# Two-operand work moved from GpSimd to VectorE in a two-layer hybrid diffusion block

## The chip, the cores and the metric

The kernel runs on one core of one Trainium2 chip. The metric is the device time of one execution in microseconds (us). The engines are called as the profile calls them: PE is TensorE (PEld its weight loads), DVE is VectorE, ACT is ScalarE, POOL is GpSimd, and SP is the engine whose queue issues most DMAs.

## What is computed

The reference runs two layers over 512 latent tokens and 256 context tokens of width 1024, each with two sub-layers that are scaled, shifted and gated by a conditioning vector:

```python
for layer in range(DEPTH):
    mod = jax.nn.silu(c) @ w_ada[layer] + b_ada[layer]        # mod_c the same from c_ctx
    sh1, sc1, gt1, sh2, sc2, gt2 = jnp.split(mod[:, None, :], 6, axis=-1)
    h = rmsnorm(x, g_norm1[layer]) * (1 + sc1) + sh1
    p = jnp.split(h @ w_in[layer], SPLIT_POINTS, axis=-1)
    ya, ya_c = window_attention(p[0:3], pc[0:3], sink_a[layer], cos, sin, need_ctx)
    yb, yb_c = dense_attention(p[3:6], pc[3:6], g_q_b[layer], g_k_b[layer], cos, sin, need_ctx)
    ym, ym_c = mlstm_mixer(p[6:11], pc[6:11], ...)
    yd, yd_c = mamba_mixer(p[11:16], pc[11:16], ...)
    x = x + gt1 * (jnp.concatenate([ya, yb, ym, yd], axis=-1) @ w_out[layer])
    h2 = rmsnorm(x, g_norm2[layer]) * (1 + sc2) + sh2
    x = x + gt2 * sq_relu_ffn(h2, w_ff1[layer], w_ff2[layer])
return rmsnorm(x, g_final)
```

The context stream goes through the same weights; in layer 1 it is only read.

## The kernel before

Activations lie with features on the 128 partitions and tokens along the free dimension. Every large product is made of three matmuls in a fast float32 format: weight and activation are each split into a rounded part and a remainder (wh and wl, h and hl, ah and al), and wh·h, wh·hl and wl·h are summed. The weights come in pieces of 256 KB (`wload`, line 165: raw piece wraw by DMA, wh by ACT, wl by DVE).

The helpers matter for reading the profile. `mm` (line 96) issues matmuls, `act` (line 104) ACT's work, and `tt`, `ts` and `stt` (lines 107, 111 or 112, 115) issue DVE's, so that many operations share a line and are told apart by the names of their tiles. What goes to POOL is written out as `G.` at its place and has a line of its own. The order on each engine is made by a scheduler from the written order, the dependencies and priorities; each engine then takes its list in order.

The stages, with their times in the profile: conditioning and first projections of layer 0 (to 66 us), windowed attention A filled with projections, the Mamba branch D, the mLSTM branch C (to about 390), dense attention B, filled with the output projection (to 506), the first feed-forward (to about 1036); then layer 1 in the same order, with its feed-forward from 1442 to about 1795. While a branch works in small steps, a generator (`Stream.fill`) puts matmuls of the next projections between them, by credits that are fixed numbers.

The places that the change touches:

- `ada_step` (line 301) makes the second layer's conditioning during the first feed-forward, one of 24 column blocks at a time. Four pieces of w_ada (tile adar, from the five ta buffers that are shared with the products adap) are loaded on SP's queue, ACT scales each row by silu(c) into adap, POOL adds them into acc (line 317), adds its two halves (line 319), and for the 16 blocks that need c alone cuts the sum into three bf16 pieces together with ACT (lines 325 and 327). `ada_finish` sums over the partitions on PE and adds the bias on DVE (tile mod). The whole step is written at the lowest priority.
- `norm_chunk` (line 402): with pool=True, every second chunk gets its shift on ACT, a rounded copy on ACT, and its remainder hl on POOL (line 408).
- `rotate` (lines 627 to 639), the rotary embedding: four ACT copies make the swapped tile qs, POOL multiplies it by the sines (line 633), DVE multiplies by the cosines, POOL adds (line 638). With g it serves branch B, without g branch A.
- `Rms` (line 360) collects sums of squares, on DVE or POOL (line 371); `row` makes a reciprocal root (`rsq`, line 184) and spreads it over the partitions with matmuls.
- `c_norm` (line 1369): the mLSTM's reciprocal roots ssC, on POOL; `c_fin` uses them (line 1376).
- The skip product of branch D (tile ysk, line 1140), on POOL.
- `whole` (line 1511): in layer 1, after the first of eight feed-forward blocks, eight products x·row of full width on POOL, then ACT and the split into h2.
- In `ffn2` the PSUM results (tiles bulk and mx, two buffers each) are added to x by DVE (x<-bulk,mod,x).

## Time and profile before

| what | value |
|---|---|
| median of 3 runs | 1813.33 us (1811.78 to 1813.99) |
| the profiled execution | 1813.98 us |
| its span, first to last instruction | 1812.2 us |
| mean granted clock of PE | 0.986 |
| POOL busy | 372.5 us, 21% of the span |
| of it ada_step's adds, halves and pieces (lines 317, 319, 325, 327) | 143.4 + 28.7 + 10.8 + 12.3 = 195.2 us |
| read from HBM | 172.51 MB, mean 98 GB/s |

A group of instructions is shown as line, engine, operation, output<-inputs, shapes, count, then busy us and mean ns of one, then the engine's idle time just ahead of them and who ended it. A line of the waits is: engine and tile that waited, <- who released it, total us, times, longest us. A line of the chain is start us, length us, engine, tile. A window row is PE, PEld, DVE, ACT and POOL busy (instructions), granted clock, DMA share and GB/s. PE's ends are modelled.

### The profile page before, as it was taken

The page shows a single profiled execution, that of the slowest core. Times are in us where ns is not written, and L with a number is a line of the kernel's source. Part 1 is how long each engine was busy: PE and PEld are TensorE (multiplying, and loading weights), DVE is VectorE, ACT ScalarE, POOL GpSimd, SP SyncE. Part 2 cuts the span into 40 slices and gives each one's busy share as a digit, 9 for nine tenths or more (in the row PEclk, how much of TensorE's full clock was granted, in tenths as well). Part 3 has the DMA queues.
Part 4 walks back from the last instruction along what each step waited for, and adds up shares of the span by engine and source line. Part 5 has one row for each costly group of instructions (what it writes and reads, how often), then busy time and mean ns, then how long its engine had stood idle before and what let it go on. Part 6 is the DMA issues. An engine that isn't in the chain of part 4 may idle for free.

```text
span 1812.2 us, 29981 instructions
## 1 busy us (share of the span) xinstructions
PE 1737.6 (96%) x11178; PEld 1505.2 (83%) x11178; DVE 1158.1 (64%) x2485; ACT 900.8 (50%) x2004; POOL 372.5 (21%) x454
## 2 busy tenths in 40 slices
PE   7999999989999999999999999999989999999997
PEld 4897998778788888888888888888868888888887
DVE  4677664588867557456456566875579884444445
ACT  4655634555666455344344455663456663333334
POOL 1300121430025344133133431012140210000001
PEclk9999999999999999999999999999999999999999
DMA  9323443241033233333333412133212132222221
GB/s 346 103 94 102 141 144 106 71 149 36 13 112 111 94 122 108 103 117 99 105 122 99 140 59 75 42 95 94 71 53 73 53 100 93 94 94 93 96 96 65
DMA packets 98833, 180.36 MB, mean 100 GB/s; under 512 B 10752, under 2 KB 19840, under 8 KB 98688
## 3 DMA queue, kind: packets, MB, share of 16 engines
q1 hardware_dynamic: 97536, 176.88, 30.2%
q0 software_dynamic: 1152, 1.57, 0.5%
q8 instruction: 88, 1.44, 0.3%
q14 instruction: 57, 0.47, 0.1%
HBM read 172.51 MB, written 4.33 MB: 98 GB/s over the span
## 4 chain that ended last, share of the span: by engine, by line
PE 75%; DVE 7%; ACT 5%; POOL 5%; DMA 4%; issue 3%; SPq 0%; POOLq 0%; ACTq 0%; DVEq 0%
PE bulk L96 36%; PE s L96 29%; PE mx L96 8%; PE mx L757 2%; DMA MB<-drows 1%; DVE wl L107 1%; ACT qs L104 1%; POOL acc L317 1%; DMA adar<-in_wada_dram 1%; ACT wh L104 1%; DMA CB<-drows 1%; DVE x L115 1%; POOL qs L633 1%; DVE m L721 0%; ACT pr L104 0%
## 5 line engine op out<-in xcount | busy, mean ns | idle before, releaser
L107 DVE TENSOR_TENSOR wl<-wraw,wh 128x512 fp32r<-128x512 f32 (+1 forms) x392 | 288.3, 742 | 138.4 <-ACT wh L104 130.6
L104 ACT ACTIVATE wh<-wraw 128x512 fp32r<-128x512 f32 (+1 forms) x392 | 239.1, 619 | 254.6 <-PE bulk L96 130.1
L96 PE MATMUL s<-h,wh 128*128 128x512 f32 (+2 forms) x848 | 291.7, 346 | 1.1 <-ACT pr L104 1.1
L96 PE MATMUL s<-hl,wh 128*128 128x512 f32 (+2 forms) x848 | 281.6, 345 | 0.2 <-DVE hl L115 0.2
L96 PE MATMUL s<-h,wl 128*128 128x512 f32 (+2 forms) x848 | 251.3, 346 | 2.3 <-DVE wl L107 2.3
L317 POOL TENSOR_TENSOR acc<-acc,adap 128x512 f32<-128x512 f32 x96 | 143.4, 1499 | 404.1 <-ACT acc L104 382.5
L96 PE MATMUL bulk<-ah,wh 128*128 128x512 f32 (+1 forms) x576 | 217.9, 378 | 4.4 <-DVE mod L107 3.7
L96 PE MATMUL bulk<-ah,wl 128*128 128x512 f32 (+1 forms) x576 | 216.1, 375 | 0.0
L96 PE MATMUL bulk<-al,wh 128*128 128x512 f32 (+1 forms) x576 | 216.0, 375 | 0.0
L115 DVE SCALAR_TENSOR_TENSOR x<-bulk,mod,x 128x512 f32<-128x512 f32 (+1 forms) x224 | 149.4, 671 | 94.3 <-PE bulk L96 93.6
L96 PEld LDWEIGHTS s<-h,wh 128*128 128x128 f32 x848 | 160.5, 189 | 30.8 <-ACT pr L104 1.5
L96 PEld LDWEIGHTS s<-hl,wh 128*128 128x128 f32 x848 | 160.6, 189 | 20.1 <-DVE hl L115 0.4
L96 PE MATMUL bulk<-h,wh 128*128 128x512 f32 (+1 forms) x416 | 155.0, 373 | 2.2 <-DVE VS L107 1.9
L96 PEld LDWEIGHTS s<-h,wl 128*128 128x128 f32 x848 | 142.9, 190 | 12.6 <-DVE wl L107 2.8
L96 PE MATMUL bulk<-hl,wh 128*128 128x512 f32 (+1 forms) x416 | 147.0, 353 | 0.0
L96 PE MATMUL bulk<-h,wl 128*128 128x512 f32 (+1 forms) x416 | 146.6, 352 | 0.0
L107 DVE TENSOR_TENSOR relu<-relu 128x512 f32<-128x512 f32 x96 | 89.4, 957 | 67.0 <-ACT relu L104 66.7
L96 PEld LDWEIGHTS bulk<-ah,wh 128*128 128x128 f32 x576 | 108.3, 188 | 26.1 <-DVE mod L107 5.8
L96 PEld LDWEIGHTS bulk<-ah,wl 128*128 128x128 f32 x576 | 108.2, 188 | 21.2
L96 PEld LDWEIGHTS bulk<-al,wh 128*128 128x128 f32 x576 | 108.2, 188 | 19.5
L104 ACT ACTIVATE adap<-adar,silw 128x256 f32<-128x256 f32 x192 | 85.1, 497 | 58.3 <-DMA adar<-in_wada_dram 58.3
L96 PE MATMUL bulk<-wh,h 128*128 128x256 f32 (+1 forms) x304 | 92.9, 306 | 4.3 <-DVE EO L107 1.7
(375 smaller groups left out, 3740.5 us busy)
## 6 DMA issues: line engine op xcount, KB each, us to landing
wraw<-in_wf_dram SPq DMA_DIRECT2D x256, 256.0 KB, 2.7
adar<-in_wada_dram SPq DMA_DIRECT2D x96, 256.0 KB, 3.0
wraw<-in_win_dram SPq DMA_DIRECT2D x80, 256.0 KB, 2.8
ada<-in_wada_dram SPq DMA_DIRECT2D x64, 256.0 KB, 4.4
adaw<-in_wada_dram SPq DMA_DIRECT2D x16, 512.0 KB, 8.8
wraw<-in_wout_dram SPq DMA_DIRECT2D x32, 256.0 KB, 3.2
x<-in_xin_dram SPq DMA_DIRECT2D x8, 768.0 KB, 5.8
CB<-drows SPq DMA_DIRECT2D x10, 512.0 KB, 6.6
```

Of the source, the lines that this page charges most:

```text
L96: return TE.matmul(o, lhsT=l, rhs=r, start=start, stop=stop)
L104: return S.activation(o, i, f, scale=scale, **kw)
L107: return V.tensor_tensor(o, a, b, op)
L115: return V.scalar_tensor_tensor(o, a, s, b, op0, op1)
L317: G.tensor_tensor(acc[:, v], acc[:, v], dst, ALU.add)
L633: G.tensor_tensor(qs, qs, rp[:, 1, :], ALU.mult)
L757: TE.transpose(tp[:, i, e, :], Ps[e][:, (i0 + i) * P:(i0 + i + 1) * P], ident)
```

## The change

In ada_step all additions and subtractions go to DVE. So do norm_chunk's remainders (the pool path is removed, with its second ACT copy), rotate's two products when there is no g (branch A), all sums of squares in Rms, c_norm's roots, and whole's products, which are now made two at a time behind each of the four column groups of the second ffn1. Three things go the other way or move: the skip product ysk is issued one block ahead, still on POOL; the scale rq of B's queries goes from DVE to POOL; and the second half's row of layer 1 (`put_row(1)`) is issued within the first block of the feed-forward, after 12 of its 32 steps, with its root on POOL.

```diff
@@ ada_step
-                        G.tensor_tensor(acc[:, v], acc[:, v], dst, ALU.add)
+                        tt(acc[:, v], acc[:, v], dst, ALU.add)
...
-                G.tensor_tensor(a, a, parts[0][0], ALU.subtract)
+                tt(a, a, parts[0][0], ALU.subtract)
@@ Rms
-        def row(self):
+        def row(self, eng=V):
             self.sums()
             r = sm((P, 4), "rc", bufs=2)[:, 0:self.nj]
-            rsq(r, self.col, 1.0 / 1024.0, EPS)
+            col = self.col
+            if eng is G:
+                col = r
+                V.tensor_copy(r, self.col)
+            rsq(r, col, 1.0 / 1024.0, EPS, eng)
@@ norm_chunk
-        if pool:
-            act(t, t, AF.Identity, bias=sh)
-            act(h[:, sl], t, AF.Copy)
-            G.tensor_tensor(lo[:, sl], t, h[:, sl].bitcast(F32), ALU.subtract)
-            return
         act(h[:, sl], t, AF.Identity, bias=sh)
         stt(lo[:, sl], t, sh, h[:, sl].bitcast(F32), ALU.add, ALU.subtract)
@@ rotate
-            G.tensor_tensor(qs, qs, rp[:, 1, :], ALU.mult)
+            eng = V if g is None else G
+            eng.tensor_tensor(qs, qs, rp[:, 1, :], ALU.mult)
...
-            G.tensor_tensor(a, a, qs, ALU.add)
+            eng.tensor_tensor(a, a, qs, ALU.add)
@@ branch D
+        skips = [d_skip(out_tok[0])]
...
+                skips.append(d_skip(out_tok[ji + 1]))
...
-            ysk = ta((P, 256), name="ysk")
+            ysk = skips[ji]
@@ rsq_b
-                    ts(rq[:, j0:NJ, 2 * m:2 * m + 2], kcs[n][:, j0:NJ, :], 0.125, None, ALU.mult)
+                    G.tensor_scalar(rq[:, j0:NJ, 2 * m:2 * m + 2], kcs[n][:, j0:NJ, :], 0.125, None, ALU.mult)
@@ c_norm
-            rsq(ssC[:, t4], ssC[:, t4], 1.0 / 64.0, EPS, G)
+            rsq(ssC[:, t4], ssC[:, t4], 1.0 / 64.0, EPS)
@@ put_row, whole, ffn1
-            row = rms[i].row()
+            row = rms[i].row(V if need or i == 0 else G)
...
-        put_row(1)
...
-                G.tensor_tensor(t, xr[c // 2][:, c % 2, LAT], rowt[0], ALU.mult)
+                tt(t, xr[c // 2][:, c % 2, LAT], rowt[0], ALU.mult)
...
+                    if b == 0 and cb == 0 and i_ == 12:
+                        put_row(1)
...
+                    if not need and b == 1:
+                        whole((4 * cb + 2 * m, 4 * cb + 2 * m + 1))
```

**First feed-forward, DVE, start of an ffn2 block.** The rows are the evictions of its first matmul groups; relu, al and wl belong to the block before and to the next weights. Before:

```order
L115 SCALAR_TENSOR_TENSOR x_4636<-bulk_10554,mod_89,x_4636 128x512
L107 TENSOR_TENSOR al_10167<-relu_10490,ah_10166 128x512
L107 TENSOR_TENSOR al_10167<-relu_10490,ah_10166 128x256
L115 SCALAR_TENSOR_TENSOR x_4636<-bulk_10568,mod_89,x_4636 128x512
L115 SCALAR_TENSOR_TENSOR x_4636<-mx_10582,mod_89,x_4636 128x256
L107 TENSOR_TENSOR wl_10786<-wraw_10787,wh_10785 128x512
L115 SCALAR_TENSOR_TENSOR x_4636<-mx_10596,mod_89,x_4636 128x256
L107 TENSOR_TENSOR wl_10792<-wraw_10793,wh_10791 128x512
L115 SCALAR_TENSOR_TENSOR x_4646<-bulk_10622,mod_89,x_4646 128x512
```

Now, where acc and adap are the conditioning sums and their scaled pieces:

```order
L115 SCALAR_TENSOR_TENSOR x_4627<-bulk_10544,mod_89,x_4627 128x512
L107 TENSOR_TENSOR al_10157<-relu_10480,ah_10156 128x512
L107 TENSOR_TENSOR al_10157<-relu_10480,ah_10156 128x256
L107 TENSOR_TENSOR acc_10513<-acc_10513,adap_10520 128x512
L107 TENSOR_TENSOR acc_10688<-acc_10688,adap_10695 128x512
L115 SCALAR_TENSOR_TENSOR x_4627<-bulk_10558,mod_89,x_4627 128x512
L107 TENSOR_TENSOR acc_10513<-acc_10513,adap_10526 128x512
L115 SCALAR_TENSOR_TENSOR x_4627<-mx_10572,mod_89,x_4627 128x256
L107 TENSOR_TENSOR acc_10513<-acc_10513,adap_10532 128x512
L107 TENSOR_TENSOR acc_10688<-acc_10688,adap_10701 128x512
L115 SCALAR_TENSOR_TENSOR x_4627<-mx_10586,mod_89,x_4627 128x256
L107 TENSOR_TENSOR wl_10776<-wraw_10777,wh_10775 128x512
```

Ahead of the second eviction stand two additions of two different steps (acc_10513 and acc_10688), and four more up to the end of the mx evictions; before, only wl and al stood between evictions.

**Layer 0, end of the mLSTM, POOL.** ys is the sum of the mLSTM's two directions, rg the temporaries of a root, ssC the norm's column, KHL the keys of B. Before:

```order
L1426 TENSOR_TENSOR ys_4788<-yc_4784 128x256
L192 TENSOR_SCALAR rg_4794<-ssC_4051 128x8
L195 TENSOR_TENSOR rg_4794<-rg_4794 128x8
L196 TENSOR_TENSOR rg_4794<-rg_4794 128x8
L204 TENSOR_SCALAR rg_4794<-rg_4794 128x8
L205 TENSOR_TENSOR rg_4794<-rg_4794 128x8
L206 TENSOR_SCALAR rg_4794<-rg_4794 128x8
L207 TENSOR_TENSOR rg_4794<-rg_4794 128x8
L208 TENSOR_TENSOR rg_4794<-rg_4794 128x8
L209 TENSOR_TENSOR rg_4794<-rg_4794 128x8
L210 TENSOR_SCALAR rg_4794<-rg_4794 128x8
L211 TENSOR_TENSOR ssC_4051<-rg_4794 128x8
```

Now (kcq and rq are the norm and scale of B's queries):

```order
L210 TENSOR_SCALAR rg_4707<-rg_4707 128x12
L211 TENSOR_TENSOR kcq_708_3667<-rg_4707 128x12
L1207 TENSOR_SCALAR rq_784<-kcq_708_3667 128x6x2
L1432 TENSOR_TENSOR ys_4779<-yc_4775 128x256
L657 DMA KHL_4856<-KHL_4856 64x2x512
L657 DMA KHL_4856<-KHL_4856 64x2x256
```

The root of ssC is no longer on POOL. It stands on DVE, as rv, ry and rw, among evictions (x), the operands EO of B, a weight remainder (wl) and the maxima m of B's scores (768 columns each):

```order
L1435 TENSOR_REDUCE ssC_4043<-sqc_4781 128x4
L107 TENSOR_TENSOR EO_4865<-qB_3662,EO_4865 64x256
L192 TENSOR_SCALAR rv_4785<-ssC_4043 128x8
L107 TENSOR_TENSOR EO_4866<-qB_3662,EO_4866 64x256
L112 TENSOR_SCALAR ry_4786<-rv_4785 128x8
L107 TENSOR_TENSOR wl_4969<-wraw_4970,wh_4968 128x512
L195 TENSOR_TENSOR rw_4787<-ry_4786 128x8
L721 TENSOR_REDUCE m_920_4876<-s_922_4878 128x1
L196 TENSOR_TENSOR rw_4787<-rw_4787,rv_4785 128x8
L721 TENSOR_REDUCE m_920_4876<-s_924_4887 128x1
L115 SCALAR_TENSOR_TENSOR rw_4787<-rw_4787 128x8
L115 SCALAR_TENSOR_TENSOR m_920_4876<-m_920_4876,rq_784 128x1 x2
```

**Start of layer 1's feed-forward, POOL.** sq are the sums of squares of the two halves, xn the products of whole, rc the root's column. Before:

```order
L371 TENSOR_TENSOR sq_16249<-sq_16249,sq_16310 128x256
L371 TENSOR_TENSOR sq_16326<-sq_16326,sq_16338 128x256
L371 TENSOR_TENSOR sq_16326<-sq_16326,sq_16351 128x256
L371 TENSOR_TENSOR sq_16326<-sq_16326,sq_16364 128x256
L1515 TENSOR_TENSOR xn_16666<-x_15100,row_16285 128x512
L1515 TENSOR_TENSOR xn_16671<-x_15100,row_16285 128x512
L1515 TENSOR_TENSOR xn_16676<-x_15110,row_16285 128x512
L1515 TENSOR_TENSOR xn_16681<-x_15110,row_16285 128x512
```

Now:

```order
L1432 TENSOR_TENSOR ys_15193<-yc_15189 128x256
L657 DMA KHL_15237<-KHL_15237 64x2x512
L657 DMA KHL_15237<-KHL_15237 64x2x256
L192 TENSOR_SCALAR rg_16417<-rc_16415 128x2
L195 TENSOR_TENSOR rg_16417<-rg_16417 128x2
L196 TENSOR_TENSOR rg_16417<-rg_16417 128x2
L204 TENSOR_SCALAR rg_16417<-rg_16417 128x2
L205 TENSOR_TENSOR rg_16417<-rg_16417 128x2
L206 TENSOR_SCALAR rg_16417<-rg_16417 128x2
L207 TENSOR_TENSOR rg_16417<-rg_16417 128x2
L208 TENSOR_TENSOR rg_16417<-rg_16417 128x2
```

The sums of squares and the eight products are gone from POOL's list, and the second half's root stands there instead.

## The prediction

> **What bounds the kernel now.** I read the page's busy shares first, then a table of windows by stage, then what TensorE (PE) waited for, then the groups of DVE and POOL instructions by shape, and last the chain of waits at the few places where PE pauses.

> ```profile
> span 1812.2 us, 29981 instructions
> PE 1737.6 (96%) x11178; PEld 1505.2 (83%) x11178; DVE 1158.1 (64%) x2485; ACT 900.8 (50%) x2004; POOL 372.5 (21%) x454
> ```

> PE is busy for 1737.6 of 1812.2 us, so about 75 us in the whole program can be given back by anything that isn't a matmul. The next table says where they lie (columns: PE, PEld, DVE, ACT, POOL busy in us).

> ```profile
> 320.00:400.00 80.00, 71.19 (x511) 61.13 (x511) 59.81 (x132) 42.66 (x96) 36.28 (x79) 0.94 0.38 118
> 513.00:1036.00 523.00, 519.33 (x3039) 452.88 (x3037) 311.09 (x498) 254.31 (x543) 194.84 (x160) 1.00 0.35 111
> 1036.00:1120.00 84.00, 76.71 (x489) 69.01 (x489) 55.52 (x114) 45.20 (x95) 24.13 (x23) 0.96 0.25 76
> 1300.00:1360.00 60.00, 52.15 (x301) 42.89 (x299) 43.02 (x91) 33.44 (x67) 27.53 (x69) 0.91 0.20 62
> 1360.00:1453.00 93.00, 86.73 (x575) 76.35 (x573) 84.58 (x193) 60.79 (x137) 17.81 (x19) 1.00 0.19 59
> 1453.00:1753.00 300.00, 299.96 (x1417) 248.91 (x1418) 159.65 (x245) 109.15 (x187) 5.72 (x4) 1.00 0.29 95
> ```

> The first feed-forward (513 to 1036), where POOL does more than half of its work, leaves PE idle for only 523.00 - 519.33 = 3.7 us. The second (1453 to 1753) leaves nothing. The pauses are at the hand-overs: 8.8 us from 320 to 400, 7.3 from 1036 to 1120, 7.9 from 1300 to 1360, 6.3 from 1360 to 1453. So the large edit stands where little can be won, and the small ones where something can.

> **First feed-forward: 96 full adds, 32 half adds and 32 subtractions go from POOL to DVE.** Groups of this stage by shape, first POOL's add (whole run), then DVE's from 560 to 1030, then DVE's from 1500 to 1740, where POOL is silent:

> ```profile
> L317 POOL TENSOR_TENSOR acc<-acc,adap 128x512 f32<-128x512 f32 x96 | 143.4, 1499 | 404.1 <-ACT acc L104 382.5
> ```
> ```profile
> L107 DVE TENSOR_TENSOR wl<-wraw,wh 128x512 fp32r<-128x512 f32 x108 | 85.2, 794 | 56.8 <-ACT wh L104 51.3 <-PE mx L96 5.5
> L115 DVE SCALAR_TENSOR_TENSOR x<-bulk,mod,x 128x512 f32<-128x512 f32 x58 | 43.1, 745 | 42.9 <-PE bulk L96 42.9
> L107 DVE TENSOR_TENSOR relu<-relu 128x512 f32<-128x512 f32 x26 | 32.1, 1236 | 16.8 <-ACT relu L104 16.6
> L107 DVE TENSOR_TENSOR al<-relu,ah 128x512 fp32r<-128x512 f32 x26 | 27.4, 1053 | 0.0
> L107 DVE TENSOR_TENSOR relu<-relu 128x256 f32<-128x256 f32 x26 | 26.8, 1029 | 0.0
> L107 DVE TENSOR_TENSOR al<-relu,ah 128x256 fp32r<-128x256 f32 x26 | 20.1, 772 | 0.0
> L107 DVE TENSOR_TENSOR relu<-s,row 128x256 f32<-128x256 f32 x26 | 10.8, 414 | 0.0
> ```
> ```profile
> L107 DVE TENSOR_TENSOR wl<-wraw,wh 128x512 fp32r<-128x512 f32 x85 | 58.6, 690 | 44.7 <-ACT wh L104 43.9
> L115 DVE SCALAR_TENSOR_TENSOR x<-bulk,mod,x 128x512 f32<-128x512 f32 x44 | 33.0, 750 | 29.0 <-PE bulk L96 29.0
> L107 DVE TENSOR_TENSOR relu<-relu 128x512 f32<-128x512 f32 x21 | 14.5, 689 | 44.4 <-ACT relu L104 44.4
> ```

> Added to DVE: 96 x 0.689 us (the relu row without POOL) + 64 x 0.414 (the 256-wide row) = 66.1 + 26.5 = 92.6 us. Given back on DVE: its own products of two SBUF operands lose POOL as a neighbour, so 26 x (1.236 - 0.689) + 26 x (1.053 - 0.689) + 26 x (1.029 - 0.414) + 26 x (0.772 - 0.414) + 108 x (0.794 - 0.690) = 14.2 + 9.5 + 16.0 + 9.3 + 11.2 = 60.2 us, in 470 of the stage's 523 us. DVE goes from 311 to about 343 us of 523, 66%, and stays off the bound. The row that proves the cause is x<-bulk,mod,x: one of its operands is in PSUM, and it takes 745 ns beside POOL and 750 without. [...]

> What it buys is bounded by what PE lost there, by the waits of that stage and of the engines that feed it:

> ```profile
> PE bulk L96 <- DVE mod L107: 3.7, 5, 1.6
> ```
> ```profile
> ACT adap L104 <- DMA adar<-in_wada_dram: 58.3, 30, 5.0
> ```

> PE's 3.7 us all end on a DVE addition that closes a conditioning step. Each sum takes under half as long (0.689 against 1.499 us), so its ta buffers come free earlier and the next adar load starts earlier; on SP's queue, where weight loads stand behind the adar loads, these then wait for DVE's release instead of POOL's. ACT's three bf16 pieces of a sum wait for DVE as they waited for POOL. I take -2.5 us, two thirds of what is there; the ends are -3.7 and the first rival below.

> **Start of layer 1 (and of layer 0).** Chain of waits from 1055 to 1115:

> ```profile
> 1060.64 1.29 POOL hl L408
> ...
> 1084.04 1.29 POOL qs L633
> 1085.39 1.31 POOL ra L638
> ...
> 1102.36 1.30 POOL qs L633
> 1103.73 1.39 POOL ra L638
> ...
> 1108.91 1.29 POOL qs L633
> 1110.27 1.63 POOL ra L638
> ```

> Three rotations spend 8.2 us on POOL in the chain; on DVE six products at 0.689 take 4.1. The remainder hl becomes DVE's own instruction at 0.75 (the x<-bulk row, of the same kind) instead of 1.29. The chain sheds 4.6 us, PE idles 7.3 us there, and DVE has room (55.5 of 84). What is late next is ACT's four qs copies ahead of each rotation, which stay. I take -3.5, between 0 and -5. In layer 0 the same edits meet a wait of PE for ACT, which now has eight copies fewer to make there:

> ```profile
> PE s L96 <- ACT h L104: 2.1, 1, 2.1
> ```

> The rest of that start is loads and statistics, so -1, between +1 and -2.

> **End of the mLSTM.** The reciprocal root of its norm leaves POOL. First and last of POOL's twelve steps in the chain (one of them on DVE), and of DVE's nine for a like column:

> ```profile
> 386.26 0.43 POOL rg L192
> ...
> 390.31 0.21 POOL ssC L211
> ```
> ```profile
> 1442.94 0.16 DVE L192 TENSOR_SCALAR rv<-mx 128x2 f32<-128x2 f32 x1 [1.28 <-PE mx L96]
> ...
> 1444.51 0.16 DVE L115 SCALAR_TENSOR_TENSOR rc<-rw,ry 128x2 f32<-128x2 f32 x1
> ```

> That is 4.3 us against 1.7 if DVE is free. It is not: in its new order other work, two maxima of the dense attention among it, stands between the nine steps, and DVE is at 43.0 of 60 us in layer 1's window. POOL's queue in turn loses those steps ahead of the rotations of B, which stay there. I take -1.5 for four such columns, between -4 and +3. The skip product of the Mamba branch, issued a block earlier, drops out of the chain twice:

> ```profile
> 1249.28 0.62 POOL ysk L1140
> ...
> 1257.87 0.59 POOL ysk L1140
> ```

> -1, between -1.2 and 0.

> **Start of layer 1's feed-forward.** Three effects. The eight whole-width products, POOL's at 1440 to 1453, move behind the first block and on to DVE; PE waited for a DVE remainder that they held up, and for POOL's sums of squares:

> ```profile
> PE s L96 <- DVE wl L107: 2.3, 1, 2.3
> PE mx L96 <- POOL sq L371: 1.3, 2, 0.7
> ```

> That is up to -3.6. Against it: the second half's root moves to POOL (up to 4.3 us by the rows above, against 1.7), while in PE's queue 15 matmuls stand between the sum and the row that needs it, where 14 stood: between 0 and +2.6. I take +1.6, since those POOL steps ran beside a busy DVE. Behind the waiting row stand PE's last matmuls of the block, and nobody else. And twelve sums of squares go to DVE, at

> ```profile
> L371 DVE TENSOR_TENSOR sq<-sq,sq 128x256 f32<-128x256 f32 x18 | 8.4, 467 | 4.1 <-ACT sq L104 4.1
> ```

> 12 x 0.467 = 5.6 us, where DVE is busy for 84.58 of 93 us; I count a third, +1.9. Together 0, between -3.6 and +4.6 (2.6 + 5.6 - 3.6). [...]

> **The sum:** -2.5 - 3.5 - 1 - 1.5 - 1 + 0 = -9.5 us. The profiled execution took 1813.98 us, its span and 1.8 around it, and 0.65 more than the median of the three runs (1813.33), which is inside their spread. 1813.98 - 9.5 = 1804.5.

> **Rivals.** 1. *DVE's one queue (slower).* The adds wait for ACT's scaled copies, and these for the adar loads: 30 waits, 58.3 us, 5.0 at most. Today POOL stands and waits; afterwards DVE does, and behind an add in its queue stand the PSUM evictions x<-bulk. The price is decided at the PSUM buffers: an eviction may be late by the other bulk tile's matmuls (half of the second row) and the mx tiles' (the first) that follow it:

> ```profile
> 872.26 2.85 PE mx L96 x24
> 875.11 5.57 PE bulk L96 x24
> ```

> That is 2.8 + 2.85 = 5.6 us, and waits of 5.0 with a few adds of 0.689 behind them pass it. If 40% of the 58.3 us reaches PE, that is +23.3 instead of -2.5, with the other terms -7.0: 1830. From 7.0 us on, an eighth of those waits, there is no gain at all. For it: the new order. Against it: loads start earlier and ACT already passes the same waits on to DVE today. [...] Chance 0.14.

> 2. *The idle time only moves.* At the hand-overs DVE is the next to be late, the more so with 5.6 us of squares and the roots. With the two terms that load it there at their bad ends (+3 for the roots, +4.6 for the feed-forward's start) and the other four at half (-4) the time is 1817.6; with those two at zero it is 1810. Chance 0.20, about 1813. For it: DVE's 84.58 of 93 us; against it: the rotations of layer 1, where DVE has room.

> 3. *More than forecast.* Matmul ends are modelled, so short pauses do not count as idle. All terms at their good ends: -3.7 - 5 - 2 - 4 - 1.2 - 3.6 = -19.5, 1794. Chance 0.10.

> **Numbers.** The forecast's own case has 0.56. The range 1793 to 1815 leaves out the first rival and a part of the second. A measurement here tells about 0.2%, 3.6 us. Faster: 0.56 + 0.10, and little of the second is left over, 0.66; same 0.20; slower 0.14.

> **What would show it.** Right: in the first feed-forward DVE's relu squares at about 0.69 us and PE idle under 3.7 us; from 1036 to 1120 a stage shorter by 3 us or more. Wrong: PE waiting for DVE x or DVE mod in the feed-forward for more than 10 us with an acc add ahead of it, or DVE over 95% from 1360 on.

## The result and the profile after

The changed kernel takes 1801.68 us (median of 4 runs, 1801.38 to 1802.57) against 1813.66 us of the kernel before (4 runs beside them): a ratio of 0.9932, 95% interval 0.9918 to 0.9946. Run again later it came to 1800.31 against 1813.5, 0.9925 (0.9905 to 0.9944). The forecast was 1804.5, with a range from 1793 to 1815. The total fits; the parts that make it do not, and most of this text is about them.

The page of the changed kernel, the span and the engines' line:

```profile
span 1799.6 us, 29869 instructions
PE 1734.9 (96%) x11178; PEld 1504.4 (84%) x11178; DVE 1184.5 (66%) x2721; ACT 896.9 (50%) x1988; POOL 113.6 (6%) x210
```

POOL lost 259 us of work and DVE gained 26. To see where time went, the two traces are laid beside each other at landmarks, the first instruction of a kind: the first bs of layer 0's feed-forward (DVE), the first xn of layer 1's norm (DVE), layer 1's load of CB in the Mamba branch (SP), its first scores of B (PE, s<-KHL,EO), and the first long run of 96 bulk matmuls in its feed-forward. The last column needs a word. The granted clock falls to half now and then, for 3.4 us at a time or two or three times as long (shown below). The column is worked out from a table of windows of 2.5 us over the whole span: the sum of length x (1 - granted clock) is what a stage lost to such drops. A drop of 3.4 us comes to 1.7 us. That is the most it can cost: where PE has little to do it costs less, as in S6, whose 4 us lie at the very end (PE works for 1.19 of the last 8.6 us of the kernel before).

| stage | before | after | difference | lost to drops, before / after |
|---|---|---|---|---|
| S1 start to first bs | 513.8 | 512.2 | -1.6 | 8.6 / 10.2 |
| S2 first feed-forward, to layer 1's xn | 544.2 | 539.1 | -5.1 | 0 / 0 |
| S3 layer 1's start, to the load of CB | 136.5 | 131.8 | -4.7 | 3.4 / 0 |
| S4 Mamba and mLSTM, to the first scores of B | 156.2 | 149.4 | -6.9 | 8.5 / 5.1 |
| S5 attention B and start of the feed-forward | 135.1 | 140.8 | +5.6 | 0 / 5.1 |
| S6 the rest | 326.3 | 326.4 | 0 | 4.3 / 4.0 |

So layer 1's two branches gained more than twice what was forecast for them, and S5, for which the forecast was zero, gave 5.6 us back.

For S2 the windows of exactly that stage, first before, then after:

```profile
513.84:1058.02 544.18, 539.30 (x3159) 470.32 (x3158) 324.26 (x526) 261.15 (x557) 198.73 (x165) 1.00 0.34 111
```
```profile
512.19:1051.28 539.09, 538.32 (x3162) 471.10 (x3161) 344.21 (x693) 262.88 (x556) 0.00 (x0) 1.00 0.35 112
```

PE's idle time was 544.18 - 539.30 = 4.9 us and is 0.8. The groups of DVE from 560 to 1020 show what its new and old work takes without POOL:

```profile
L107 DVE TENSOR_TENSOR wl<-wraw,wh 128x512 fp32r<-128x512 f32 x108 | 73.3, 687 | 35.9 <-ACT wh L104 30.5 <-PE mx L96 5.4
L107 DVE TENSOR_TENSOR acc<-acc,adap 128x512 f32<-128x512 f32 x84 | 56.6, 686 | 8.3 <-ACT adap L104 7.9
L107 DVE TENSOR_TENSOR relu<-relu 128x512 f32<-128x512 f32 x26 | 18.0, 692 | 5.1 <-ACT relu L104 4.6
```

The relu square takes 692 ns (1236 before, 689 forecast), an add 686. The waits of the whole run hold, among others, two of PE in S5, the first of them new and the second 0.5 us before, and the one that the first rival rested on:

```profile
PE mx L96 <- POOL rc L211: 3.0, 1, 3.0
PE bulk L96 <- ACT yS L104: 1.7, 1, 1.7
ACT adap L104 <- DMA adar<-in_wada_dram: 72.1, 36, 4.5
```

The waits for the adar loads have grown, from 58.3 to 72.1 us, and none is seen to reach PE: in S2 it waits once, 0.7 us for an eviction x, and no longer for mod.

**What a drop is.** Windows of 1 us of the changed kernel, around the wait for yS (each row: length, then PE, PEld, DVE, ACT and POOL busy, granted clock, DMA share, GB/s):

```profile
1413.00:1414.00 1.00, 0.76 (x7) 0.67 (x6) 0.21 (x2) 0.31 (x2) 0.00 (x0) 1.00 0.22 82
1414.00:1415.00 1.00, 0.00 (x0) 0.00 (x0) 0.92 (x5) 0.00 (x0) 0.00 (x0) 1.00 0.00 0
1415.00:1416.00 1.00, 0.50 (x2) 0.30 (x2) 0.90 (x6) 0.42 (x1) 0.00 (x0) 1.00 0.00 0
1416.00:1417.00 1.00, 0.98 (x5) 0.98 (x6) 0.64 (x4) 0.08 (x1) 0.00 (x0) 0.60 0.00 0
1417.00:1418.00 1.00, 1.00 (x7) 1.00 (x7) 1.00 (x3) 1.00 (x3) 0.00 (x0) 0.50 0.00 0
1418.00:1419.00 1.00, 1.00 (x6) 1.00 (x6) 0.98 (x3) 1.00 (x4) 0.00 (x0) 0.50 0.00 0
1419.00:1420.00 1.00, 1.00 (x8) 1.00 (x7) 0.91 (x3) 0.23 (x1) 0.00 (x0) 0.69 0.59 203
1420.00:1421.00 1.00, 1.00 (x11) 1.00 (x10) 0.74 (x2) 0.92 (x2) 0.00 (x0) 1.00 0.16 59
```

PE pauses for 1.7 us, works again at 1415.5, and from 1416.2 its clock is 0.50 until 1419.6: 0.40 + 0.50 + 0.50 + 0.31 = 1.7 us of work lost, when PE is busy again. In the drop the matmuls of yS with 256 columns start 0.21 us apart (1416.26, 1416.47 and 1416.68 us), behind it matmuls of 258 columns 0.12 us (1420.00, 1420.12 and 1420.24). This pause of 1.7 us costs its own length and then as much once more. What decides whether a drop follows is worked out at the end of the experiments.

### The profile page after: what moved, and what is told of

Same layout as the page of the kernel before. It is cut to its first block, busy times and chain, and to the rows that moved or that the text cites. A ratio compares the mean times of both kernels' runs of the same rounds, so it can differ in the third digit from the quotient of the medians.

```text
span 1799.6 us, 29869 instructions
## 1 busy us (share of the span) xinstructions
PE 1734.9 (96%) x11178; PEld 1504.4 (84%) x11178; DVE 1184.5 (66%) x2721; ACT 896.9 (50%) x1988; POOL 113.6 (6%) x210
## 5 line engine op out<-in xcount | busy, mean ns | idle before, releaser
L104 ACT ACTIVATE wh<-wraw 128x512 fp32r<-128x512 f32 (+1 forms) x392 | 240.5, 621 | 276.6 <-PE bulk L96 134.0
L107 DVE TENSOR_TENSOR wl<-wraw,wh 128x512 fp32r<-128x512 f32 (+1 forms) x392 | 265.9, 684 | 115.7 <-ACT wh L104 108.2
L96 PE MATMUL s<-h,wh 128*128 128x512 f32 (+2 forms) x848 | 292.1, 347 | 1.8 <-ACT pr L104 1.1
L96 PE MATMUL s<-hl,wh 128*128 128x512 f32 (+2 forms) x848 | 282.5, 346 | 0.0
L96 PE MATMUL s<-h,wl 128*128 128x512 f32 (+2 forms) x848 | 251.3, 346 | 0.0
L96 PE MATMUL bulk<-ah,wh 128*128 128x512 f32 (+1 forms) x576 | 217.4, 377 | 0.7 <-DVE x L115 0.7
L96 PE MATMUL bulk<-ah,wl 128*128 128x512 f32 (+1 forms) x576 | 216.1, 375 | 0.0
L96 PE MATMUL bulk<-al,wh 128*128 128x512 f32 (+1 forms) x576 | 215.9, 375 | 0.0
L115 DVE SCALAR_TENSOR_TENSOR x<-bulk,mod,x 128x512 f32<-128x512 f32 (+1 forms) x224 | 150.0, 672 | 93.4 <-PE bulk L96 92.8
L96 PEld LDWEIGHTS s<-h,wh 128*128 128x128 f32 x848 | 161.1, 190 | 31.6 <-ACT pr L104 1.6
L96 PEld LDWEIGHTS s<-hl,wh 128*128 128x128 f32 x848 | 161.3, 190 | 20.1 <-issue 0.6
L96 PE MATMUL bulk<-h,wh 128*128 128x512 f32 (+1 forms) x416 | 153.6, 369 | 1.8 <-DVE VS L107 1.5
L96 PEld LDWEIGHTS s<-h,wl 128*128 128x128 f32 x848 | 143.6, 190 | 9.7
L96 PE MATMUL bulk<-hl,wh 128*128 128x512 f32 (+1 forms) x416 | 145.5, 350 | 0.0
L96 PE MATMUL bulk<-h,wl 128*128 128x512 f32 (+1 forms) x416 | 144.8, 348 | 0.0
L96 PEld LDWEIGHTS bulk<-ah,wl 128*128 128x128 f32 x576 | 108.2, 188 | 21.2
L96 PEld LDWEIGHTS bulk<-ah,wh 128*128 128x128 f32 x576 | 108.3, 188 | 20.5 <-DVE x L115 0.8
L96 PEld LDWEIGHTS bulk<-al,wh 128*128 128x128 f32 x576 | 108.2, 188 | 19.8
L104 ACT ACTIVATE adap<-adar,silw 128x256 f32<-128x256 f32 x192 | 86.0, 499 | 73.5 <-DMA adar<-in_wada_dram 72.1
L96 PE MATMUL bulk<-wh,h 128*128 128x256 f32 (+1 forms) x304 | 93.0, 306 | 2.7 <-DVE ra L107 2.1
L107 DVE TENSOR_TENSOR relu<-relu 128x512 f32<-128x512 f32 x96 | 54.9, 600 | 54.1 <-ACT relu L104 53.6
L96 PEld LDWEIGHTS bulk<-h,wh 128*128 128x128 f32 x416 | 79.8, 192 | 12.2 <-issue 2.3
```

The costliest lines, as they stand in the source:

```text
L96: return TE.matmul(o, lhsT=l, rhs=r, start=start, stop=stop)
L104: return S.activation(o, i, f, scale=scale, **kw)
L107: return V.tensor_tensor(o, a, b, op)
L115: return V.scalar_tensor_tensor(o, a, s, b, op0, op1)
```

## The experiments

The theory was the prediction's: a sum of separate terms, in which POOL is slow and in the way, so that what leaves it pays by the length of its steps. Against it stood the rivals of each part: contention or latency in S2, an edit's gain given back in the next stage, and later a coupling of two edits through DVE's queue. Kernels called "before with" hold one edit alone; "changed with" is the changed kernel with one edit undone or altered. Each was timed beside runs of the kernel before on the same chip (medians 1812.08 to 1813.5 us). "Less drops" is S4 and S5 with what the drops took subtracted. A profile is one execution; the last column is the mean over all executions of a kernel, worked out from the span and the mean granted clock of each: span x (1 - clock) as the drops, and the span less them.

| kernel | median us | ratio to before (95%) | S2 | S3 | S4 | S5 | S4, S5 less drops | all executions: drops, span less drops |
|---|---|---|---|---|---|---|---|---|
| before | 1813.66 | 1 | 544.2 | 136.5 | 156.2 | 135.1 | 147.7, 135.1 | 24.8 to 25.4, 1785.5 to 1786.7 |
| before with the conditioning on DVE | 1808.36 | 0.9978 (0.9966 to 0.9989) | 539.1 | 135.0 | 155.1 | 136.2 | 146.5, 134.5 | 26.9, 1780.2 |
| before with A's rotation on DVE | 1810.56 | 0.9996 (0.9983 to 1.001) | 542.1 | 133.5 | 156.1 | 136.2 | 147.6, 134.6 | 25.5, 1783.9 |
| before with the early skip | 1811.73 | 0.999 (0.9978 to 1.0002) | 542.9 | 135.0 | 153.0 | 135.2 | 147.8, 135.2 | 25.2, 1784.4 |
| before with the mLSTM root on DVE | 1817.11 | 1.0028 (1.0013 to 1.0042) | 543.0 | 134.6 | 153.6 | 141.0 | 148.4, 135.9 | 26.1, 1789.4 |
| changed | 1801.68 | 0.9932 (0.9918 to 0.9946) | 539.1 | 131.8 | 149.4 | 140.8 | 144.3, 135.6 | 24.8, 1775.3 |
| changed, repeated | 1800.31 | 0.9925 (0.9905 to 0.9944) | 539.1 | 131.9 | 150.9 | 139.1 | 144.1, 134.0 | 22.2, 1775.7 |
| changed with the conditioning on POOL | 1803.84 | 0.9956 (0.9941 to 0.9971) | 542.9 | 131.8 | 147.7 | 139.4 | 144.3, 135.9 | 23.4, 1778.7 |
| changed with idle POOL products | 1796.32 | 0.9903 (0.9888 to 0.9918) | 539.1 | 131.8 | 147.6 | 139.5 | 144.2, 136.1 | 19.7, 1774.3 |
| changed with the second row's root on DVE | 1801.35 | 0.9938 (0.9921 to 0.9955) | 539.2 | 131.8 | 146.8 | 138.8 | 145.1, 135.4 | 23.7, 1775.9 |
| changed with that and the row at its old place | 1799.71 | 0.9926 (0.9914 to 0.9939) | 539.1 | 131.8 | 147.8 | 138.7 | 144.3, 135.3 | 23.7, 1774.5 |
| changed with that root on DVE, squares on POOL | 1797.48 | 0.9914 (0.9897 to 0.993) | 539.1 | 131.9 | 151.1 | 135.2 | 144.3, 133.5 | 22.5, 1773.5 |
| changed with the mLSTM root on POOL | 1802.86 | 0.9942 (0.9927 to 0.9958) | 539.1 | 131.8 | 151.6 | 138.0 | 146.5, 134.6 | 22.5, 1778.4 |
| changed with the query scale on DVE | 1810.43 | 0.9987 (0.9974 to 1.0001) | 539.1 | 132.0 | 154.5 | 143.3 | 147.7, 134.8 | 30.5, 1778.4 |

S4 of the same code runs from 146.8 to 151.1 us, but without drops from 144.1 to 145.1: the scatter is drops.

### The first feed-forward

The conditioning's four additions and subtractions back on POOL in the changed kernel, and alone on DVE in the kernel before:

```diff
-                        tt(acc[:, v], acc[:, v], dst, ALU.add)
+                        G.tensor_tensor(acc[:, v], acc[:, v], dst, ALU.add)
...
```

> The changed kernel with ada_step's additions and subtractions back on POOL, all else as changed. Theory (the change's gain is a sum of separate terms, and the first feed-forward gave about 4 of the 12 us): 1805.5 us, 0.9955 of the kernel before, DVE's relu products of 512 columns near 1.24 us again, PE waiting again some 3 to 4 us for DVE mod in the first feed-forward. Rival A (DVE's one queue costs something there and another stage pays for it): at or under 1801.7. Rival B (the gain is a luck of the new order on the engines, not of the engine that adds): within 1.5 us of 1801.7.

> The kernel before with only ada_step's additions and subtractions on DVE. Theory: 1809.5 us, 0.9977 of the kernel before (4 us, what PE waited in the first feed-forward and a little that the modelled ends hide); PE waits there under 1 us. Rival A: 1813 or slower. Rival B: anywhere from 1805 to 1816, with the first feed-forward as long as before.

S2 takes 542.1 to 544.2 us in the five kernels with these sums on POOL and 539.1 or 539.2 in the nine with them on DVE, in either company: this edit alone makes S2's gain, 3.0 to 5.1 us, and 1812.08 - 1808.36 = 3.7 us of the total by itself (less drops 1785.7 - 1780.2 = 5.5). The window of S2 with the conditioning back on POOL:

```profile
510.40:1053.27 542.87, 539.49 (x3163) 470.80 (x3162) 325.56 (x533) 262.00 (x558) 194.14 (x160) 1.00 0.34 111
```

PE idles 3.4 us again, 2.6 of them for DVE's mod, and the relu squares take 1233 ns again. Was it POOL's presence (contention) or the slowness of its sums? The third kernel keeps the sums on DVE and gives POOL work that nobody waits for:

```diff
+            for v in range(nv):
+                for _ in range(7):
+                    G.tensor_tensor(acc[:, v, 1, :], acc[:, v, 1, :], acc[:, v, 1, :], ALU.subtract)
         ada_state["pend"] = (cb, parts)
```

> The changed kernel, with 7 POOL subtractions of 128x256 behind each of the 32 conditioning sums of the first feed-forward, on a half of the sum that is no longer read: POOL is as busy as it was before (about 190 us), but nobody needs what it computes. The first feed-forward (first bs of layer 0 to first xn of layer 1) took 544.2 us before and 539.1 changed, while TensorE's visible waits there came to only 3.7 us. Theory contention (DVE's two-SBUF-operand instructions are held up by POOL's, and that reaches TensorE): DVE's relu squares go back to over 1 us, and the stage takes 542 us or more, the total 3 to 5 us more than the changed kernel. Theory latency (POOL's long chain of adds made each conditioning step late): the relu squares go back to over 1 us all the same, but the stage stays at 538.5 to 540 and the total within 2 us of the changed kernel.

Its S2 window, and two of DVE's groups from 560 to 1020:

```profile
510.12:1049.18 539.06, 538.29 (x3162) 471.07 (x3161) 373.55 (x692) 264.07 (x558) 169.81 (x224) 1.00 0.35 112
```
```profile
L107 DVE TENSOR_TENSOR wl<-wraw,wh 128x512 fp32r<-128x512 f32 x108 | 80.7, 757 | 27.1 <-ACT wh L104 22.4 <-PE mx L96 4.6
L107 DVE TENSOR_TENSOR relu<-relu 128x512 f32<-128x512 f32 x25 | 19.2, 767 | 5.8 <-ACT relu L104 5.6
```

With 169.8 us of POOL work beside it DVE is 29.3 us busier (373.55 against 344.21), and S2 does not change by 0.1 us. So the gain was the latency of the sums, 686 ns an add on DVE against 1499 on POOL in the kernel before. One reservation: the relu squares rose to 767 ns only, not over 1 us as both theories had expected, perhaps because these products stand in bunches elsewhere than the sums did, which was not tried; DVE's 29.3 us are about half of the 60.2 that the prediction counted as contention, so half of it was there, not all. The median, 1796.3, is below the changed kernel's; most of that is drops, of which its four executions had fewer (19.7 us in the mean against 24.8 and 22.2; less drops 1774.3 against 1775.3 and 1775.7), and its interval touches that of the changed kernel and overlaps that of its repetition. Nothing is concluded from it.

### Layer 1's start

```diff
-            G.tensor_tensor(qs, qs, rp[:, 1, :], ALU.mult)
+            eng = V if g is None else G
+            eng.tensor_tensor(qs, qs, rp[:, 1, :], ALU.mult)
...
```

> The kernel before with only branch A's two rotation products on DVE. Theory (the POOL pairs were on the path at the start of layer 1): 1810 us, 0.998 of the kernel before, with the 3.5 us won between the end of the first feed-forward and layer 1's first scores of A. Rival (ACT's four copies ahead of each rotation set the pace): 1813, no change.

S3 falls from 136.5 to 133.5, near what the theory had, and the total does not show it. The 136.5 us hold two drops; the kernel with the rotation has none there. In the kernel with the mLSTM root alone, whose S3 has the old code and no drop, it is 134.6, and in two others with the old code and one drop it is 135.0. So the rotation's own work is worth 134.6 - 133.5 = 1.1 us, and the other 1.9 are drops that did not come. In the changed kernel S3 is 131.8 to 132.0 in all nine profiles that have its code there, without a drop in eight of them. The ninth, at 132.0, has one, which cost it 0.2 us at most: in S3 1.7 us for a drop is too much, and the comparison of profiles without drops is the safer one. The 1.7 us from 133.5 to 131.8 must be the other edits of that stage, the remainders hl and ACT's copies among them, which were not tried alone.

### The end of the mLSTM, and the edit without a price

The two edits to which the prediction gave S4's gain, each alone:

```diff
+        skips = [d_skip(out_tok[0])]
...
-            ysk = ta((P, 256), name="ysk")
+            ysk = skips[ji]
```

> The kernel before, with the skip product of the Mamba branch issued one block earlier and nothing else. From the load of CB in layer 1 to the first scores of B it took 156.2 us before and 149.4 changed, 6.9 us less, of which the prediction gave about 1 to this edit. Theory A (the skip product, whose POOL step stood in the chain twice, is 1 to 1.3 us): 155 to 155.5. Rival (it also holds up W and so the 2.8 us wait of TensorE for DVE W): 153 or less. The total is within 2 us of the kernel before by theory A.

```diff
-            rsq(ssC[:, t4], ssC[:, t4], 1.0 / 64.0, EPS, G)
+            rsq(ssC[:, t4], ssC[:, t4], 1.0 / 64.0, EPS)
```

> The kernel before, with the reciprocal root of the mLSTM's norm (twelve POOL steps of 128 x few) on DVE and nothing else. Theory A (this root is most of the gain in the end of layer 1's mLSTM, since the 3.1 us wait of TensorE for DVE yc goes with it): CB load to the first scores of B in layer 1 takes 152 to 153.5 us against 156.2 before, and the wait for yc is gone. Rival (the root is 1.5 us or nothing, and the gain came of the skip product and the query scale that left DVE): 154.5 to 157.

The skip shortens S4 by 3.3 us, as its rival had it, and the root by 2.7, as theory A had it. But less drops S4 is 147.8 and 148.4 against 147.7: the gain is drops that did not come in those executions, and the skip's total shows nothing beyond its interval. Some of PE's waits in S4, of the kernel before, with the skip and with the root, tell why there is no more:

```profile
PE s L96 <- DVE W L107: 3.1, 2, 2.8
PE s L96 <- DVE yc L107: 3.1, 1, 3.1
```
```profile
PE s L96 <- DVE yc L107: 3.1, 1, 3.1
PE mx L1161 <- ACT yD L104: 2.4, 1, 2.4
PE s L96 <- DVE W L107: 0.5, 1, 0.5
```
```profile
PE s L96 <- DVE W L107: 3.3, 2, 3.1
PE s L96 <- DVE EO L107: 2.3, 1, 2.3
PE s L96 <- DVE rw L196: 1.9, 1, 1.9
```

The skip turns the wait for W into one for yD. With the root the matmul that waited 3.1 us for yc (s<-SC,qT) waits 1.9, now until the root's step rw just behind yc, so that this wait is shorter but not gone as theory A had it, and the wait for EO grows from 1.1 us to 2.3. PE idles for 12.4 us in S4 before, 12.2 with the skip and 11.9 with the root; in the changed kernel it is 8.5. The root alone makes the kernel slower, 1.0028, and over all executions that is not drops (26.1 us against 25.3 beside them) but 3.9 us of work (1789.4 against 1785.5). In the profile S5 is 5.9 us longer with it, 5.1 of them in three drops, one behind a pause of 1.9 us for yS that is 0.5 in the kernel before. First and last step of one such root on DVE in this kernel:

```profile
1344.76 0.17 DVE L192 TENSOR_SCALAR rv<-ssC 128x8 f32<-128x8 f32 x1
...
1350.62 0.15 DVE L115 SCALAR_TENSOR_TENSOR ssC<-rw,ry 128x8 f32<-128x8 f32 x1
```

The nine steps of 0.15 to 0.17 us take 6.0 us, longer than POOL's 4.3, because other work stands between them. Back on POOL in the changed kernel:

> The changed kernel, with the reciprocal root of the mLSTM's norm back on POOL and nothing else. Theory A (on DVE its nine steps stand between other work and took 11.3 and 5.5 us in layer 1, against 4.3 to 5.2 on POOL; TensorE then waits 1.7 us for ACT yS later and its clock drops; the edit gave its early gain back): first scores of B to the second block of layer 1's feed-forward falls from 139.5-140.8 to 135.5-137.5, and from the load of CB to there it takes 1 to 4 us less than changed. Rival (the root on DVE is worth the 2.7 us that it won ahead of the scores of B): from the load of CB to there it takes 1 to 3 us more than changed.

The total is 1802.86 against 1800.31 on the same chip, with ratios that overlap, and from the load of CB on S4 and S5 take 289.6 against 290.0: neither the gain of theory A nor the loss of its rival is there. Less drops S4 is 146.5 against 144.1, so the root is worth 2.4 us there in this company (2.7 over all executions, 1778.4 against 1775.7) and less than nothing alone. What makes the company is in DVE's waits, in S4 of the kernel before, and of it with the root alone on DVE:

```profile
DVE rq L111 <- POOL kcq L211: 5.2, 2, 3.7
```
```profile
DVE rq L111 <- POOL kcq L211: 4.8, 2, 2.4
```

rq, one product of 128x8, scales the query norms by 0.125. On DVE it waits for POOL's root kcq, and everything behind it in DVE's list waits too. The change moves it to POOL, behind that very root. Undone:

```diff
-                    G.tensor_scalar(rq[:, j0:NJ, 2 * m:2 * m + 2], kcs[n][:, j0:NJ, :], 0.125, None, ALU.mult)
+                    ts(rq[:, j0:NJ, 2 * m:2 * m + 2], kcs[n][:, j0:NJ, :], 0.125, None, ALU.mult)
```

> The changed kernel, with the scaling of the query norms (rq, one 128x8 product per branch) back on DVE and nothing else. In the traces so far a drop of the granted clock to 0.50 lasts about 3.4 us and takes 1.7 us of TensorE's work; with those drops taken off, the stretch from the load of CB to the first scores of B in layer 1 takes 147.7 us before, 144.1 to 145.1 in six kernels that have all the edits there, but 147.8 with the early skip product alone, 148.4 with the mLSTM root alone on DVE, and 146.5 with all but that root. Theory (this edit is what lets the root on DVE pay: in DVE's queue rq stands waiting for POOL's root kcq, 5.2 us in two waits before and 4.8 with the root alone on DVE, and the mLSTM root's steps stand behind it): with rq back on DVE those waits are back at 4 us or more, and the stretch takes 146.5 to 148.5 us without the drops. Rival (the edits' gains simply add, and this one is worth nothing): 144 to 145.3 us, whether DVE waits or not.

The theory's numbers came out: the wait is back, S4 less drops is 147.7, and the total is 1810.43, 10 us more than the changed kernel. That kernel's waits of DVE in S4, and its DVE around the second wait (start, length, instruction, idle before it):

```profile
DVE rq L111 <- POOL kcq L211: 4.8, 2, 2.5
```
```profile
1331.64 0.74 DVE L115 SCALAR_TENSOR_TENSOR x<-bulk,mod,x 128x512 f32<-128x512 f32 x1
1334.78 0.17 DVE L111 TENSOR_SCALAR rq<-kcq 128x8 f32<-128x8 f32 x1 [2.39 <-POOL kcq L211]
1334.86 0.16 DVE L107 TENSOR_TENSOR den<-den,E 128x8 f32<-128x8 f32 x1
1334.93 0.68 DVE L107 TENSOR_TENSOR yc<-yc,s 128x512 f32<-128x512 f32 x1
```

The same place in the changed kernel:

```profile
1327.88 0.67 DVE L107 TENSOR_TENSOR yc<-yc,s 128x512 f32<-128x512 f32 x1
1328.48 0.15 DVE L115 SCALAR_TENSOR_TENSOR den<-den 128x8 f32<-128x8 f32 x1
1328.56 0.74 DVE L115 SCALAR_TENSOR_TENSOR x<-bulk,mod,x 128x512 f32<-128x512 f32 x1
1329.22 0.15 DVE L107 TENSOR_TENSOR den<-den,E 128x8 f32<-128x8 f32 x1
```

den and yc of the mLSTM, which need nothing of kcq, stood behind rq for 2.4 us, and so did a step of the mLSTM's root (rw) at the first wait, of 2.5 us. PE idles for 11.2 us in S4 of this kernel, against 8.5 and 8.9 in the two profiles of the changed one. By stages against the changed kernel of the first trace, S1 is 1.8 us longer, S4 5.2 and S5 2.5; S1 less drops is 505.4, as in the kernel before (505.3), against 501.9, so that layer 0's gain hangs on this edit too. The larger part of the 10 us is drops: over all executions they take 30.5 us, against 24.8 and 22.2 in the changed kernel, and less drops the kernel takes 1778.4 us against 1775.3 and 1775.7, about 3 us more. That the waits bring the drops, since they make PE pause, is likely but not shown pause by pause. Whether rq alone in the kernel before would bring as much was not tried.

### The start of layer 1's feed-forward

```diff
-            row = rms[i].row(V if need or i == 0 else G)
+            row = rms[i].row(V)
```

> The changed kernel with the reciprocal root of layer 1's second half on DVE instead of POOL. Theory (POOL's root of 4.4 us holds up PE's row, 3.0 us of wait): 1799.3 us, 0.9920 of the kernel before, and PE's wait for the row under 0.8 us. Rival (the weights and DVE's evictions behind the row are late anyway): 1801.5, with the wait moved to the next matmul.

In place of 3.0 us for POOL's rc PE waits, in this kernel:

```profile
PE mx L96 <- DVE rc L115: 1.6, 1, 1.6
```

S5 is 138.8 against 139.1 to 140.8 in the four profiles with that root on POOL: 0.9 less than their mean, 139.7, and less drops the same (135.4 against a mean of 135.4). Neither the total of the theory (1799.3) nor its wait under 0.8 us came. Next, with that root on DVE, the row at its old place, and, in another kernel, the squares on POOL:

```diff
             if i == 0:
                 put_row(0)
+        put_row(1)
...
-                    if b == 0 and cb == 0 and i_ == 12:
-                        put_row(1)
```

> The changed kernel, with the second half's norm row of layer 1 at its old place (ahead of the feed-forward's first matmuls, not behind twelve of them) and its root on DVE. From the first scores of B to the second block's 96 matmuls of layer 1's feed-forward: 135.1 us before, 140.8 changed, 138.8 changed with the root on DVE. Theory squares (the twelve sums of squares on DVE cost the rest, wherever the row stands): 138 to 139.5. Rival place (the row at its new place makes TensorE wait in the middle of the block's first matmuls, and the granted clock drops behind it): 135 to 136.5.

```diff
-        rms = [Rms(fsegs[0][0].stop - fsegs[0][0].start, 4, V, tf, True),
-               Rms(256, 4, V, ta)]
+        rms = [Rms(fsegs[0][0].stop - fsegs[0][0].start, 4, V if need else G, tf, True),
+               Rms(256, 4, V if need else G, ta)]
```

> The changed kernel, with layer 1's twelve sums of squares back on POOL and the second half's root on DVE. First scores of B to the second block of layer 1's feed-forward: 140.8 changed, 138.8 with the root alone on DVE. Theory squares (their 5.6 us on a DVE that is busy for nine tenths of the time count): 136 to 137.5. Rival (DVE's squares lie beside other work): 138 to 139.5.

The row's place makes no difference (138.7 and 138.8). The squares do: 135.2, as in the kernel before and a little better than their theory expected. PE's waits in S5 of that kernel, the first three:

```profile
PE bulk L96 <- ACT yS L104: 1.9, 1, 1.9
PE bulk L96 <- DVE x L115: 1.8, 2, 1.5
PE mx L96 <- POOL sq L371: 1.0, 2, 0.6
```

The wait for the root is gone and the wait for yS is not. Of the 3.6 us, 1.7 are one drop and 1.9 work. This is the best of the versions that follow from the experiments (1797.48, 0.9914), but its interval overlaps the changed kernel's beside it, so it isn't shown to beat it.

Do drops follow from waits? The wait for wl was there before, 2.29 us up to 1453.04, with no drop behind it. In the kernel with the conditioning alone on DVE PE waits as long at the same place:

```profile
1448.89 0.38 PE L96 MATMUL s<-h,wl 128*128 128x258 f32 x1 [2.29 <-DVE wl L107]
```
```profile
1447.50:1450.00 2.50, 1.11 (x7) 1.11 (x8) 2.50 (x2) 1.63 (x3) 2.50 (x3) 0.91 0.02 7
1450.00:1452.50 2.50, 2.50 (x14) 2.50 (x13) 2.50 (x3) 0.51 (x1) 2.50 (x2) 0.50 0.29 105
1452.50:1455.00 2.50, 2.50 (x21) 2.50 (x21) 2.50 (x2) 2.50 (x7) 2.05 (x2) 0.91 0.00 0
```

and here the clock is at 0.50 in the second of these windows. Five profiles have this same pause of 2.3 us, and three of them a drop behind it. So its length alone does not decide. Where it falls does: in each of the fourteen traces all drops begin on one grid, and all but the last, which runs into the end of the trace, last one to three whole steps of it. In the kernel before they begin at 25.27, 83.30, 332.47 and 376.85 us and so on, 17, 73 and 13 steps of 3.413 us apart. On this grid the pause lies with 2.29, 2.29 and 1.96 us inside one step in the three profiles with a drop; in the two without, the step boundary divides it into 1.30 + 0.99 (the kernel before) and 1.75 + 0.54. All steps of the fourteen traces that ran at full clock, from just behind PE's start to the last drop, by PE's idle time in the step:

| PE idle in the step | steps | a drop in the next step |
|---|---|---|
| under 1 us | 6827 | 6 |
| 1 to 1.75 us | 227 | 51 |
| 1.75 us or more | 69 | 67 |

So whether a pause of about 2 us costs 1.7 us more depends on where it falls on the grid, which differed between these five profiles.

## Why the prediction came out

**The first feed-forward (-2.5).** Right in its mechanism, too small: -5.1, in the kernel with the edit alone too, whose median gave -3.7. The idle time was read from 513 to 1036, where it was 3.7 us; the stage goes on to 1058, and over all of it the idle time was 4.9, of which 0.8 is left. The two thirds had no ground. The forecast for DVE, 343 us of 523, came out as 332.5. That the gain came through latency and not through DVE's faster products is what the prediction had said of the waits for mod, and the idle products of POOL showed it.

**The first rival (DVE's one queue, 1830)** fell where it was put: ACT's waits for the adar loads grew to 72.1 us and PE waited for none of them. Its mechanism was at work elsewhere, and before the change: rq on DVE waits in a list in order, for 5.2 us in S4. In the changed kernel with rq back on DVE den and yc stood 2.4 us behind an rq of 0.17 us. There rq on DVE costs 10 us, about 3 of them work and the rest drops.

**Layer 1's start (-3.5).** -4.7, and the stage from 1036 to 1120 is shorter by more than 3 us, as was said. The window of that stage in the changed kernel:

```profile
1036.00:1120.00 84.00, 78.98 (x550) 71.97 (x548) 62.06 (x146) 46.59 (x98) 1.16 (x2) 1.00 0.23 69
```

The granted clock was 0.96 in this window before and is 1.00. By the profile with the old code and no drop (134.6), 1.9 of the 4.7 us are drops that no longer happen, a term that the prediction did not have, and 2.8 are work. Of the 4.1 us that the chain of waits gave to the rotation on POOL, 1.1 were PE's to win.

**The end of the mLSTM (-1.5), the skip product (-1) and layer 0's start (-1): the step that failed.** The sum of the three was -3.5; S1 and S4 gave -8.5, and -6.8 less drops. The root was priced by the length of its own steps and by what stands between them, and the skip by its place in the chain; neither is shown to bring anything alone, because PE's pauses moved to the next late input (11.9 and 12.2 us idle in S4, against 12.4). The edit of this place that got no price at all, rq, decides: on DVE it takes 10 us from the changed kernel, with the drops. The wait that shows it stood in the trace of the kernel before, among DVE's own waits, which the prediction does not use: it goes by PE's waits, the groups and the chain.

**The start of layer 1's feed-forward (0, at worst +4.6).** +5.6 in the first trace and +4.5 as the mean of the four profiles with the same code there (139.7). Less drops it is 135.6, 134.0, 136.1 and 135.9 against 135.1: the terms for waits and squares did nearly cancel. What came on top is two or three drops, 3.4 to 5.1 us, two of them right behind the new pauses of 1.7 and 3.0 us, in the windows at 1415 and 1435. POOL's root cost 0.9 (forecast 1.6), all of it drops; the squares 1.9 in work (forecast 1.9) and a drop, so that of their 5.6 us on DVE a third counted.

So the total was right, within 2.8 us, by errors that cancel: S1 to S4 brought 18.3 us where 9.5 was forecast, and S5 gave 5.6 back where none was. That it came so near is luck; that it came out faster is not, since less drops the changed kernel takes 1775.3 and 1775.7 us against 1785.5 to 1786.7, 10 to 11 us less. The second rival, that idle time only moves, describes S5 and the two single edits in S4 well, but not the total.

## What to carry to other kernels

Read the waits of every engine that works in order, not only those of the bound one: a tiny instruction that waits there holds up all that stands behind it, and its price follows from the wait, not from its length (rq took 0.17 us, and den and yc stood 2.4 us behind it). Two edits at one place need not add; test each alone and each taken away. Where PE pauses for 1 us or more within 3.4 us, count the drop of the clock that may follow (here behind 118 of 296 such steps of the grid) as a term of its own, and compare kernels with the drops taken off, by stage and over all executions.
